# Average pooling by four: one 32 KB store for every two 64 KB loads

## The chip, the core and the metric

The kernel runs on one core of a Trainium2 chip. Its engines used here are VectorE (DVE in the profile), ScalarE (ACT) and SyncE (SP, which only issues DMAs); 16 DMA engines move data between HBM and the core's on-chip memory, SBUF, which has 128 partitions. The metric is the device time of one execution in microseconds, the median of several runs. Sizes such as "64 KB" are per partition; a 64 KB load is 128 x 64 KB = 8.389 MB, and a 16 KB store is 2.097 MB.

## The reference

The input is float32 of shape (64, 256, 8192), and every four neighbouring numbers are replaced by their mean; kernel size and stride are both 4:

```
out_len = (length - kernel_size) // stride + 1
for i in range(out_len):
    start = i * stride
    output[:, :, i] = np.mean(x[:, :, start : start + kernel_size], axis=2)
```

The output has shape (64, 256, 2048). 536.87 MB are read and 134.22 MB written, and nothing is used twice. Since 8192 is a multiple of 4, no window crosses a row, and the whole input can be treated as one flat array.

## The kernel before

The flat input is cut into blocks. A block of width w covers 128 x w neighbouring numbers, of which partition p gets the p-th run of w, so that a load of 64 KB a partition reads one solid stretch of 8.389 MB in HBM. There are 63 blocks of 16384 numbers a partition, and the last 16384 are cut into five blocks of 8192, 4096, 2048, 1280 and 768, which share one input buffer and one result buffer. In this text, load 0 to load 62 are the full blocks, and the pieces are the five small ones (the tail).

There are two input buffers of 64 KB (`xin`) and four result buffers of 16 KB (`res`), 192 KB in all.

For each block, `load` (line 62) issues one DMA on SP's queue. `means` then runs two additions on VectorE: line 71 adds even and odd neighbours, in place, into the first half of the input buffer; line 72 adds even and odd neighbours of those sums into the result buffer. ScalarE then multiplies the result by 1/4 in place (line 80); only for the last piece VectorE does that (line 76). `store` (line 85) issues a DMA of the result.

The loop runs over the blocks in order and issues load i + 1 before the sums of block i. Because there are two input buffers, load i + 1 can begin only when line 72 has read the last of block i - 1. The loads of all five pieces are issued together, once load 61's buffer is free. Most stores are issued by ScalarE itself, right behind the multiplication; the stores of load 62 and of the first piece are issued by SP, behind all the loads. No engine order is written out by hand beyond this program order; semaphores that the framework inserts hold an instruction until its operands are ready, and until a buffer's last reader is done.

Queue q1 in the profile holds what SP issues, and q10 what ScalarE issues.

Of the kernel before, what the change touches and what calls it, by code (L numbers as in the profile page):

```python
# [1 line left out]

# [4 lines left out]


FULL = 16384
BUFS_IN = 2  # L10
BUFS_OUT = 4

HEAD = ()
TAIL = (8192, 4096, 2048, 1280, 768)


@with_exitstack
def kernel(
    ctx: ExitStack,
    tc: tile.TileContext,  # L20
    x: bass.AP,
    kernel_size: bass.AP,
    stride: bass.AP,
    out: bass.AP,
):
    nc = tc.nc
    K, S = int(kernel_size), int(stride)
    assert K == S == 4
    B, C, L = x.shape
    assert L % K == 0  # L30
    P = nc.NUM_PARTITIONS
    dt = x.dtype
    add = mybir.AluOpType.add


    xf = x.rearrange("b c l -> (b c l)")
    of = out.rearrange("b c l -> (b c l)")
    rest = B * C * L // P - sum(HEAD) - sum(TAIL)
    assert rest % FULL == 0
    blocks = [(w, i == 0) for i, w in enumerate(HEAD)]  # L40
    blocks += [(FULL, True)] * (rest // FULL)
    blocks += [(w, i == 0) for i, w in enumerate(TAIL)]
    n = len(blocks)
    first = n - len(TAIL)

    pin = ctx.enter_context(tc.tile_pool(name="xin", bufs=BUFS_IN))
    pout = ctx.enter_context(tc.tile_pool(name="res", bufs=BUFS_OUT))

    xs, begins = {}, [0]
    for w, _ in blocks:  # L50
        begins.append(begins[-1] + w)

    def load(i):

        w, fresh = blocks[i]
        if fresh:
            load.tile, load.at = pin.tile([P, FULL], dt, name="xt"), 0
        a = load.at
        load.at += w
        src = xf[P * begins[i] : P * begins[i + 1]].rearrange("(p m) -> p m", p=P)  # L60
        xs[i] = load.tile[:, a : a + w]
        nc.sync.dma_start(out=xs[i], in_=src)  # L62

    def means(i):
        w, fresh = blocks[i]
        if fresh:
            means.tile, means.at = pout.tile([P, FULL // K], dt, name="ot"), 0
        a = means.at
        means.at += w // K
        o, xt = means.tile[:, a : a + w // K], xs.pop(i)  # L70
        nc.vector.tensor_tensor(out=xt[:, : w // 2], in0=xt[:, ::2], in1=xt[:, 1::2], op=add)  # L71
        nc.vector.tensor_tensor(  # L72
            out=o, in0=xt[:, : w // 2 : 2], in1=xt[:, 1 : w // 2 : 2], op=add
        )
        if i == n - 1:
            nc.vector.tensor_scalar(  # L76
                out=o, in0=o, scalar1=1.0 / K, scalar2=None, op0=mybir.AluOpType.mult
            )
        else:
            nc.scalar.mul(o, o, 1.0 / K)  # L80
        return o

    def store(engine, i, o):
        dst = of[P * begins[i] // K : P * begins[i + 1] // K]
        engine.dma_start(out=dst.rearrange("(p m) -> p m", p=P), in_=o)

    loaded = 0
    for i in range(n):

        while loaded < n and (loaded < i + BUFS_IN or loaded > first):  # L90
            load(loaded)
            loaded += 1
        o = means(i)

        store(nc.sync if i in (first - 1, first) else nc.scalar, i, o)


# [1 line left out]
_INS = ['x', 'kernel_size', 'stride']  # L99
_OUTS = [((64, 256, 2048), 'float32')]  # L100

_NUMBERS = {'kernel_size': 4, 'stride': 4}


# [26 lines left out]
```

## Time and profile before

| | us |
|---|---|
| time, median of 3 runs (1555.77 to 1555.85) | 1555.82 |
| the profiled execution's own time | 1555.85 |
| its span, first to last instruction | 1554.1 |
| VectorE busy | 840.5 |
| ScalarE busy | 233.1 |
| waits of VectorE on loads, in total | 700.5 |

In the profile, "L71" is line 71. A group's line has the engine, the operation, output and input with their shapes, the count, the busy time and the mean of one instruction in nanoseconds, and then the idle time of the engine before these instructions and what ended it. In the timeline and in the chain of waits, the first number of a line is the start in microseconds and the second the duration. A DMA's line has its size, and the time from its issue to its landing. Part 3 of the page gives, for a queue, packets, megabytes and the share of the 16 DMA engines' time that its packets took.

### The profile page before, as it was taken

The numbers are of one execution on the slowest core, as the hardware profiler recorded it, in microseconds if no ns is written. First come the engines' busy times: TensorE is split into PE (matmuls) and PEld (weight loads), VectorE is DVE, ScalarE is ACT, GpSimd is POOL, SyncE is SP. The second block draws the span as 40 slices with busy tenths as digits, with TensorE's granted clock in tenths as the row PEclk, the third lists the DMA queues.
The fourth block names the chain that finished last, engine by engine and source line by source line (L and its number), as shares of the span: only waits on it lengthen the run. The fifth ranks groups of instructions, "written<-read, shape, count | busy, mean of one in ns | idle before, by whom it ended". The sixth has DMA issues, their size and how long they took to land.

```text
span 1554.1 us, 576 instructions
## 1 busy us (share of the span) xinstructions
DVE 840.5 (54%) x137; ACT 233.1 (15%) x68; POOL 0.2 (0%) x4
## 2 busy tenths in 40 slices
DVE  3646556465464554645546455464554645646557
ACT  1111110110101101011011110111101111011111
POOL 0000000000000000000000000000000000000000
DMA  9999999999999999999999999999999999999999
GB/s 420 416 433 439 439 439 439 427 422 433 439 439 439 436 423 428 434 439 439 437 437 416 434 436 439 439 437 430 420 435 437 439 439 435 431 421 434 438 439 385
DMA packets 19589, 671.14 MB, mean 432 GB/s; under 512 B 2176, under 2 KB 2432, under 8 KB 2944
## 3 DMA queue, kind: packets, MB, share of 16 engines
q1 hardware_dynamic: 10080, 540.02, 80.3%
q10 hardware_dynamic: 9504, 131.08, 19.7%
q14 instruction: 5, 0.04, 0.0%
HBM read 536.87 MB, written 134.22 MB: 432 GB/s over the span
## 4 chain that ended last, share of the span: by engine, by line
DMA 72%; DVE 27%; issue 0%; DVEq 0%; SPq 0%
DMA xt<-in_x_dram 72%; DVE xt L71 18%; DVE ot L72 9%; DVEq L72 0%; SPq L62 0%; DVE ot L76 0%
## 5 line engine op out<-in xcount | busy, mean ns | idle before, releaser
L71 DVE TENSOR_TENSOR xt<-xt 128x8192 f32<-128x8192 f32 (+2 forms) x68 | 556.8, 8190 | 700.5 <-DMA xt<-in_x_dram 700.5
L80 ACT ACTIVATE ot<-ot 128x4096 f32<-128x4096 f32 (+2 forms) x67 | 231.8, 3461 | 1312.8 <-DVE ot L72 1312.8
L72 DVE TENSOR_TENSOR ot<-xt 128x4096 f32<-128x4096 f32 (+2 forms) x68 | 283.8, 4175 | 6.0 <-DVE xt L71 0.5
L80 ACT ACT_TABLE_LOAD x1 | 1.3, 1283 | 0.7 <-PEq L112 0.7
L76 DVE TENSOR_SCALAR ot<-ot 128x192 f32<-128x192 f32 x1 | 0.3, 261 | 0.0
L112 POOL MEMSET const-bfloat16-1.0<- 128x1 bf16 x1 | 0.1, 101 | 0.0
L112 POOL MEMSET const-uint8-127<- 128x1 uint8 x1 | 0.1, 101 | 0.0
L112 POOL MEMSET const-float32-0.0<- 128x1 f32 x1 | 0.1, 98 | 0.2 <-issue 0.2
L112 POOL MEMSET const-float32-1.0<- 128x1 f32 x1 | 0.1, 98 | 0.0
## 6 DMA issues: line engine op xcount, KB each, us to landing
out_dram<-ot ACTq DMA_DIRECT2D x62, 2048.0 KB, 31.6
xt<-in_x_dram SPq DMA_DIRECT2D x1, 4096.0 KB, 25.5
xt<-in_x_dram SPq DMA_DIRECT2D x1, 2048.0 KB, 30.1
out_dram<-ot SPq DMA_DIRECT2D x1, 2048.0 KB, 13.4
xt<-in_x_dram SPq DMA_DIRECT2D x1, 1024.0 KB, 32.1
out_dram<-ot SPq DMA_DIRECT2D x1, 1024.0 KB, 10.5
xt<-in_x_dram SPq DMA_DIRECT2D x63, 35.1
xt<-in_x_dram SPq DMA_DIRECT2D x1, 640.0 KB, 33.8
```

Of the source, the lines that this page charges most:

```text
L71: nc.vector.tensor_tensor(out=xt[:, : w // 2], in0=xt[:, ::2], in1=xt[:, 1::2], op=add)
L72: nc.vector.tensor_tensor(out=o, in0=xt[:, : w // 2 : 2], in1=xt[:, 1 : w // 2 : 2], op=add)
L76: nc.vector.tensor_scalar(out=o, in0=o, scalar1=1.0 / K, scalar2=None, op0=mybir.AluOpType.mult)
L80: nc.scalar.mul(o, o, 1.0 / K)
L112: nc = _bacc.Bacc("TRN2", target_bir_lowering=False, num_devices=1)
```

## The change

The first 62 loads are grouped in pairs. A pair covers 128 x 32768 neighbouring numbers, and partition p has a run of 32768 of them, 128 KB: the pair's first load reads the first 64 KB of every partition's run, the second load the second 64 KB. Input buffers and the two additions of each load stay as they are. Both loads of a pair write their sums into the two halves of one result buffer of 32 KB; after the second, one ScalarE instruction scales the whole of it, and one DMA stores 32 KB a partition, from ScalarE's queue. There are two such result buffers instead of four of 16 KB, so the memory used is the same 192 KB.

Load 62 stays single, with its own scaling and its store on SP's queue. The last 16384 numbers are one group as well: each partition has a run of 64 KB, and it is loaded in four pieces of 8192, 4096, 2560 and 1536 numbers, instead of five solid blocks. The four pieces are scaled and stored one by one, the first on SP's queue, the rest on ScalarE's; the last is again scaled by VectorE.

That is 67 loads instead of 68, and 36 stores instead of 68.

```
-BUFS_IN = 2
-BUFS_OUT = 4
+PAIR = 2
-TAIL = (8192, 4096, 2048, 1280, 768)
+TAIL = (8192, 4096, 2560, 1536)
...
+    sizes = [PAIR] * ((loads - 2) // PAIR)
+    sizes += [1] * (loads - PAIR * len(sizes))
+    begins = [sum(sizes[:g]) * FULL for g in range(len(sizes))]
+    pin = ctx.enter_context(tc.tile_pool(name="xin", bufs=2))
+    pout = ctx.enter_context(tc.tile_pool(name="res", bufs=2))
+
+    def part(flat, g, k):
+        a, n = begins[g] // k, sizes[g] * FULL // k
+        return flat[P * a : P * (a + n)].rearrange("(p m) -> p m", p=P)
+
+    def load(g, a, xt):
+        nc.sync.dma_start(out=xt, in_=part(xf, g, 1)[:, a : a + xt.shape[1]])
+
+    def store(engine, g, ot, a, b):
+        engine.dma_start(out=part(of, g, K)[:, a:b], in_=ot[:, a:b])
+
+    def sums(xt, o):
+        w = xt.shape[1]
         nc.vector.tensor_tensor(out=xt[:, : w // 2], in0=xt[:, ::2], in1=xt[:, 1::2], op=add)
         nc.vector.tensor_tensor(
             out=o, in0=xt[:, : w // 2 : 2], in1=xt[:, 1 : w // 2 : 2], op=add
         )
...
+    full = [(g, l) for g, n in enumerate(sizes[:-1]) for l in range(n)]
+    xs = {}
+
+    def fetch(i):
+        g, l = full[i]
+        xs[i] = pin.tile([P, FULL], dt, name="xt")
+        load(g, l * FULL, xs[i][:, :])
+
+    tail = len(sizes) - 1
+    edges = [sum(TAIL[:i]) for i in range(len(TAIL) + 1)]
+    fetch(0)
+    for i, (g, l) in enumerate(full):
+        if i + 1 < len(full):
+            fetch(i + 1)
+        else:
+            xt = pin.tile([P, FULL], dt, name="xt")
+            for a, b in zip(edges[:-1], edges[1:]):
+                load(tail, a, xt[:, a:b])
+        if l == 0:
+            ot = pout.tile([P, PAIR * FULL // K], dt, name="ot")
+        o = ot[:, l * FULL // K : (l + 1) * FULL // K]
+        sums(xs.pop(i)[:, :], o)
+        if l == sizes[g] - 1:
+            o = ot[:, : sizes[g] * FULL // K]
+            nc.scalar.mul(o, o, 1.0 / K)
+            queue = nc.sync if i == len(full) - 1 else nc.scalar
+            store(queue, g, ot, 0, sizes[g] * FULL // K)
+
+    ot = pout.tile([P, PAIR * FULL // K], dt, name="ot")
+    for i, (a, b) in enumerate(zip(edges[:-1], edges[1:])):
+        o = ot[:, a // K : b // K]
+        sums(xt[:, a:b], o)
+        if i == len(TAIL) - 1:
+            nc.vector.tensor_scalar(out=o, in0=o, scalar1=1.0 / K, scalar2=None, op0=mult)
         else:
             nc.scalar.mul(o, o, 1.0 / K)
+        store(nc.sync if i == 0 else nc.scalar, tail, ot, a // K, b // K)
```

More of the change, by code (lines that the diff above doesn't have):

```diff
@@ L9 @@
 FULL = 16384
-BUFS_IN = 2
-BUFS_OUT = 4
-HEAD = ()
-TAIL = (8192, 4096, 2048, 1280, 768)
+PAIR = 2
+TAIL = (8192, 4096, 2560, 1536)
 @with_exitstack
@@ L32 @@
     dt = x.dtype
-    add = mybir.AluOpType.add
+    add, mult = mybir.AluOpType.add, mybir.AluOpType.mult
     xf = x.rearrange("b c l -> (b c l)")
     of = out.rearrange("b c l -> (b c l)")
[L38 to L70, printed above, removed]
+    loads = B * C * L // P // FULL
+    assert loads * P * FULL == B * C * L and sum(TAIL) == FULL
+    sizes = [PAIR] * ((loads - 2) // PAIR)
[12 more added lines that the diff above has]
+        w = xt.shape[1]
         nc.vector.tensor_tensor(out=xt[:, : w // 2], in0=xt[:, ::2], in1=xt[:, 1::2], op=add)
@@ L74, in means @@
         )
[L75 to L78, printed above, removed]
+    full = [(g, l) for g, n in enumerate(sizes[:-1]) for l in range(n)]
[29 more added lines that the diff above has]
+            nc.vector.tensor_scalar(out=o, in0=o, scalar1=1.0 / K, scalar2=None, op0=mult)
         else:
             nc.scalar.mul(o, o, 1.0 / K)
[L81 to L95, printed above, removed]
+        store(nc.sync if i == 0 else nc.scalar, tail, ot, a // K, b // K)
 _INS = ['x', 'kernel_size', 'stride']
```

## The prediction

> **What bounds the kernel now.** I read the page's summary first, then the groups of instructions by shape, the waits, the start of the timeline, the DMA issues and the end of the chain.
>
> ```profile
> span 1554.1 us, 576 instructions
> DVE 840.5 (54%) x137; ACT 233.1 (15%) x68; POOL 0.2 (0%) x4
> q1 hardware_dynamic: 10080, 540.02, 80.3%
> q10 hardware_dynamic: 9504, 131.08, 19.7%
> HBM read 536.87 MB, written 134.22 MB: 432 GB/s over the span
> ```
>
> VectorE works 54% of the span, ScalarE 15%; the two DMA queues together take 80.3 + 19.7 = 100% of the 16 DMA engines. q1 holds SP's transfers (68 loads and two stores), q10 ScalarE's 66 stores. A DMA leaves 128 packets, one a partition row, and 16 small ones: 66 x 144 = 9504, 70 x 144 = 10080. So each DMA engine handles 8 rows of a load or store.
>
> ```profile
> DVE xt L71 <- DMA xt<-in_x_dram: 700.5, 64, 22.8
> L71 DVE TENSOR_TENSOR xt<-xt 128x8192 f32<-128x8192 f32 x63 | 547.6, 8692 | 699.1 <-DMA xt<-in_x_dram 699.1
> L72 DVE TENSOR_TENSOR ot<-xt 128x4096 f32<-128x4096 f32 x63 | 278.8, 4426 | 5.9 <-DVE xt L71 0.5
> L80 ACT ACTIVATE ot<-ot 128x4096 f32<-128x4096 f32 x63 | 227.8, 3616 | 1305.3 <-DVE ot L72 1305.3
> ```
>
> VectorE needs 8.69 + 4.43 = 13.1 us for a load, then waits on the next. No row has VectorE waiting for a result buffer.
>
> ```profile
> 22.76 8.69 DVE L71 TENSOR_TENSOR xt<-xt 128x8192 f32<-128x8192 f32 x1 [22.76 <-DMA xt<-in_x_dram]
> 35.95 3.62 ACT L80 ACTIVATE ot<-ot 128x4096 f32<-128x4096 f32 x1 [33.94 <-DVE ot L72]
> 42.09 8.69 DVE L71 TENSOR_TENSOR xt<-xt 128x8192 f32<-128x8192 f32 x1 [6.17 <-DMA xt<-in_x_dram]
> 1494.02 8.69 DVE L71 TENSOR_TENSOR xt<-xt 128x8192 f32<-128x8192 f32 x1 [10.98 <-DMA xt<-in_x_dram]
> 1518.21 8.69 DVE L71 TENSOR_TENSOR xt<-xt 128x8192 f32<-128x8192 f32 x1 [10.99 <-DMA xt<-in_x_dram]
> ```
>
> L71 starts as its load lands, so distances between starts are prices. Loads 0 to 1, before any store: 42.09 - 22.76 = 19.33 us for 8.389 MB, 434 GB/s. Loads 61 to 62, one store among them: 24.19 us for 10.486 MB, 433 GB/s; the commonest distance in the whole timeline is 24.18. Reads alone and reads with writes run at one rate: bytes are the bound. The page's rate has dips (427 and 422 in slices 7 and 8) that the landings don't have: the chain's steps there start at 284.28 and 332.64, two loads in 48.36 us.
>
> ```profile
> out_dram<-ot ACTq DMA_DIRECT2D x1, 2048.0 KB, 27.2
> out_dram<-ot ACTq DMA_DIRECT2D x62, 2048.0 KB, 31.6
> ```
>
> The first store (issues between 38 and 58 us) lands after 27.2 us, though its bytes alone are worth 4.85 us. That fits packets of the two queues taking turns: eight rounds of a 64 KB load row (19.33 / 8 = 2.42 us) and a 16 KB store row (0.61) are 24.2, and 3.0 are start and completion. At the median of 31.6, each store outlives the 24.2 us to the next one: the store queue is never empty.
>
> ```profile
> 1507.25 25.49 DMA xt<-in_x_dram
> 1532.77 4.44 DVE xt L71
> 1546.81 0.26 DVE ot L76
> out_dram<-ot ACTq DMA_DIRECT2D x1, 96.0 KB, 6.1
> ```
>
> At the end VectorE works without a break from 1532.77 to 1547.07, but the DMA engines still move 403 GB/s between 1543.6 and 1551.0: the last stores' bytes set the end. The last store, issued near 1547.1, lands 6.1 us later; on an emptier queue it would need about the 3.0 above, so VectorE is some 3 us early.
>
> **The change part by part**, against the profiled execution: span 1554.1, its time 1555.85, 1.75 outside the span; the median shown is 1555.82, so a change of the span is put onto that.
>
> *31 merged stores.* With c the time of 16 KB on an engine, o a packet's fixed cost, s that of completion: 32c + 8o + s = 19.33 and 8c + 8o + s = 24.18 - 19.33 = 4.85. So 24c = 14.48, 8c = 4.827, and a store's fixed cost on the engines is 0.023 us. 31 x 0.023 = 0.7 us saved. With the mean distance, (1518.21 - 42.09) / 61 = 24.20, the fixed cost is 0.05: 1.5 saved. On the other side, load 62 to the tail's first piece (eight rows each of 32 and 16 KB) took 1532.77 - 1518.21 = 14.56 where 3 x 4.827 + 2 x 0.023 = 14.53 was due; such an excess with every pair would cost 1 us. Ends: -1.5 and +1; taken -0.7, from the row that recurs some sixty times.
>
> The Trainium skill, page "DMA: Bandwidth & Descriptors", section "Anatomy of one DMA", gives a DMA issued from GpSimd a fixed 2.0 us beside its bytes. Charged to the 33 DMAs that go here (136 to 103), that would be 66 us, a time near 1490; the 0.023 above says that queued DMAs hide it, and I go by that row.
>
> *ScalarE.* 31 pairs of 3.62 us become 31 instructions on 128x8192: from 1.911 (2048 wide) to 3.616 (4096) a step costs 1.705, so 3.62 + 2 x 1.705 = 7.03 us. Busy time hardly moves; ScalarE idles 85%. The cost is delay: a pair's store is issued 13.1 + 7.0 = 20.1 us after its second load lands, its first half's bytes a load later than before. Behind the instruction ScalarE has only the store that needs it. Nothing, as long as the queues hold work.
>
> *Does the load queue hold work?* When no store is in flight a load takes 19.33 us, and the load after it is issued 13.1 us after its predecessor landed: 6.2 us to spare, of which a start with completion takes 22.76 - 0.73 - 19.33 = 2.7. 3.5 us are left. The start of this trace shows the case: load 2, issued behind load 0's sums, was behind load 1 without a gap (42.09 to 66.64 is 24.55 with a store among it). Nothing; without that cover each microsecond of gap costs 31 us.
>
> *Two result buffers of 32 KB.* A pair's store moves eight rounds of 64 and 32 KB: 8 x (2.42 + 1.21) = 29.0, plus 3.0: landed 20.1 + 32.0 = 52 us after the pair's second load. The buffer is written again by the pair after next, at L72 of its first load: three loads later (about 72.5) plus 8.7, 81 us. 29 us to spare: nothing.
>
> At the tail it is tight. The tail's buffer is that of the last pair. With T the landing of load 61, that store is issued at T + 20.1; load 62 lands near T + 21; from there 32 KB store rows alternate with the first piece's 32 KB rows, 8 x 2.42 = 19.4, so both finish near T + 41 and the store is known to have landed near T + 43. The piece's L72 comes at T + 41 + 4.4 = T + 45.5. 2 us to spare; a wait of up to 2 would eat into VectorE's 3 us. Nothing, bound +2.
>
> *The tail in four.* Old sums: 14.40 us of instructions. New, by interpolating the rows: 6.72 and 3.51 for the first two pieces, 1.48 + 0.82 for 2560, 0.95 + 0.55 for 1536, 0.45 for the scaling on VectorE: 14.48. VectorE ends 0.1 us later, under the stores. SP's order stays: four loads, then the store of load 62, then that of the first piece, each waiting on ScalarE with nothing behind. When the last load row lands, 4.19 MB of stores remain, as before: 9.7 us of DMA in both. One load and one store fewer: 0.05 us.
>
> *Loads from 128 KB rows.* 62 loads now read 64 KB of every 128 KB instead of one solid block. No row shows that. The nearest rows: 16 KB store rows at that pitch (431 GB/s), 32 KB at 32 (14.56 us above, 432), 64 KB at 64 (434): two doublings with no loss, so I take nothing. As upper end I charge each load the worst excess of one distance in the trace, 24.60 against 24.18: 62 x 0.42 = 26 us. On the other side a gain beyond 434 GB/s isn't seen anywhere.
>
> The same page, section "Latency and other measured facts", speaks against this part: rows at 512 KiB pitch gave 207 GB/s per direction, at 4 MiB 103, padded 214. Our pitch is below its list, so as written it charges nothing; read as a 3.3% loss that begins here, it would make 63 x 19.33 = 1218 us of loads 40 us longer, about 1595.
>
> Sum: -0.7 - 0.05 + 0.0, so a span near 1553.3 and 1555.1 by the median.
>
> **The rivals.**
> - *Doubled read pitch* (the slower side). For: it is the one thing the trace has no row for. Against: no loss over two doublings. It decides from a load longer by 3.1 / 62 = 0.05 us; at the bound, 1555.1 + 26 = 1581.
> - *The load queue runs dry once in a pair.* For: load-only phases are new. Against: 3.5 us of cover, and load 2. At 1 us of gap: 1555.1 + 31 = 1586.
> - *The tail's buffer wait.* It decides when the wait passes 3 us by the 3.1 that count: from 6 us; at 8, 1555.1 + 5 = 1560.
> - *Faster.* With every byte at 434 GB/s, 671.09 MB take 1546.3; with the head (22.76 - 19.33 = 3.4) and 2.2 for the last landing the span is 1551.9, the time 1553.6. More than 0.2% would need a rate that no row has.
> - *32 KB rows split into 16 KB packets,* so that the merge saves nothing: 1555.8. The packet count tells.
>
> **How the numbers follow.** 0.2%, 3.1 us, is about what can be told from no change: 1552.7 to 1558.9 is "same". The forecast with the split and small tail waits: 0.74, its own range 1553.5 to 1557. Pitch 0.14, dry queue 0.03, tail 0.03: slower 0.20. Faster 0.06. The range from 1552.5 to 1566 leaves out most of the 0.06 and about two thirds of the pitch and queue cases, some 0.17.
>
> **What would show it.** Packets 19589 down to 14837 (q10 34 x 144 = 4896, q1 69 x 144 = 9936). Distances between L71 starts alternate, near 20.5 and 27.8, summing to 48.3 a pair. The ScalarE group reads 128x8192, x31, about 7.0 us; a store of 4096 KB lands in about 32 us. No wait of L72 on a store but perhaps one at the tail, under 2 us. Wrong if the first two loads land over 19.4 us apart (pitch), if a pair's sum exceeds 48.5, or if the engines idle between pieces at the end.

## The result, and the profile after

The changed kernel takes 1571.32 us (1569.45 to 1571.62), the kernel before 1555.84: a ratio of 1.0097, 95% interval 1.0079 to 1.0114. It became 15.5 us slower, 1.0%, where no change was forecast. The profiled execution took 1571.62, its span is 1569.8.

The summary and the two DMA queues of the changed kernel's page:

```profile
span 1569.8 us, 477 instructions
DVE 840.7 (54%) x135; ACT 226.5 (14%) x36; POOL 0.2 (0%) x4
DMA packets 14835, 671.12 MB, mean 428 GB/s; under 512 B 1648, under 2 KB 1776, under 8 KB 2160
q1 hardware_dynamic: 9936, 540.02, 80.4%
q10 hardware_dynamic: 4896, 131.07, 19.3%
HBM read 536.87 MB, written 134.22 MB: 427 GB/s over the span
```

Work and bytes are the same and the DMA engines are as busy as before, but the rate over the span fell from 432 to 427 GB/s. The rows did arrive as 32 KB packets: 4896 records on q10 and 9936 on q1, as counted ahead.

Its groups by shape, its waits and a line of its DMA issues:

```profile
L60 DVE TENSOR_TENSOR xt<-xt 128x8192 f32<-128x8192 f32 x63 | 547.6, 8693 | 711.7 <-DMA xt<-in_x_dram 711.7
L61 DVE TENSOR_TENSOR ot<-xt 128x4096 f32<-128x4096 f32 x63 | 278.8, 4425 | 3.8
L91 ACT ACTIVATE ot<-ot 128x8192 f32<-128x8192 f32 x31 | 217.9, 7029 | 1308.5 <-DVE ot L61 1308.5
```
```profile
DVE xt L60 <- DMA xt<-in_x_dram: 716.1, 65, 22.9
DVE ot L61 <- DMA out_dram<-ot: 1.1, 1, 1.1
```
```profile
out_dram<-ot ACTq DMA_DIRECT2D x31, 4096.0 KB, 33.2
```

Nothing was added on an engine: VectorE waits 716.1 us for loads instead of 700.5, and these 15.6 us are the whole loss. No buffer is late but the tail's, by 1.1 us. So the loads come later, and the timeline tells where (L60 starts as its load lands; ACTq is the issue of a store):

```profile
22.87 8.69 DVE L60 TENSOR_TENSOR xt<-xt 128x8192 f32<-128x8192 f32 x1 [22.87 <-DMA xt<-in_x_dram]
42.21 8.69 DVE L60 TENSOR_TENSOR xt<-xt 128x8192 f32<-128x8192 f32 x1 [6.19 <-DMA xt<-in_x_dram]
61.56 8.69 DVE L60 TENSOR_TENSOR xt<-xt 128x8192 f32<-128x8192 f32 x1 [6.20 <-DMA xt<-in_x_dram]
...
627.63 8.69 DVE L60 TENSOR_TENSOR xt<-xt 128x8192 f32<-128x8192 f32 x1 [15.30 <-DMA xt<-in_x_dram]
647.87 0.34 ACTq L56 DMA_DIRECT2D out_dram<-ot  x1
648.15 8.69 DVE L60 TENSOR_TENSOR xt<-xt 128x8192 f32<-128x8192 f32 x1 [7.37 <-DMA xt<-in_x_dram]
676.82 8.69 DVE L60 TENSOR_TENSOR xt<-xt 128x8192 f32<-128x8192 f32 x1 [15.47 <-DMA xt<-in_x_dram]
```

The first three landings, before any store, are 19.34 and 19.35 us apart although they read 64 KB of every 128 KB: reads alone have lost nothing. Then the distances alternate. 648.15 - 627.63 = 20.52 is a load (19.33) and one 32 KB store row (1.21), and from 250 us on such short distances recur within a few hundredths. The load with the other seven store rows should take 19.33 + 8.47 = 27.8; it took 28.67 here and between 28.05 and 28.86 elsewhere from 250 us on. From load 3 (89.16) to load 61 (1508.22) the mean of a pair is 1419.06 / 29 = 48.93 us, where 2 x 24.18 = 48.36 was the price before: 0.57 a pair, 17 us over the 31 pairs (the total lost 15.5). The loss is in the load into which a store starts. In this text a *start* is a store that begins on a queue that stood empty.

The trace's DMA packet records put it more narrowly. A load row of 64 KB takes 2.42 us on its engine; in the kernel before, 65 of 8064 took over 0.03 us longer. In the changed kernel 586 did, with an excess of 14.5 us per engine (before: 1.3), most of it within 5 us of a store's first rows. The later rows, taking turns with store rows, run at 2.42 again.

### The profile page after: what moved, and what is told of

The parts are those of the page before. It is cut to its first block, busy times and chain, and to the rows that moved or that the text cites. A ratio compares the mean times of both kernels' runs of the same rounds, so it can differ in the third digit from the quotient of the medians.

```text
span 1569.8 us, 477 instructions
## 1 busy us (share of the span) xinstructions
DVE 840.7 (54%) x135; ACT 226.5 (14%) x36; POOL 0.2 (0%) x4
## 3 DMA queue, kind: packets, MB, share of 16 engines
q1 hardware_dynamic: 9936, 540.02, 80.4%
q10 hardware_dynamic: 4896, 131.07, 19.3%
## 4 chain that ended last, share of the span: by engine, by line
DMA 73%; DVE 26%; issue 0%; SPq 0%
DMA xt<-in_x_dram 73%; DVE xt L60 17%; DVE ot L61 9%; SPq L53 0%; DVE ot L101 0%
## 5 line engine op out<-in xcount | busy, mean ns | idle before, releaser
L60 DVE TENSOR_TENSOR xt<-xt 128x8192 f32<-128x8192 f32 (+2 forms) x67 | 556.8, 8310 | 716.1 <-DMA xt<-in_x_dram 716.1
L91 ACT ACTIVATE ot<-ot 128x8192 f32<-128x8192 f32 (+1 forms) x32 | 221.5, 6923 | 1322.1 <-DVE ot L61 1322.1
L103 ACT ACTIVATE ot<-ot 128x2048 f32<-128x2048 f32 (+2 forms) x3 | 3.7, 1235 | 11.4 <-DVE ot L61 11.4
## 6 DMA issues: line engine op xcount, KB each, us to landing
out_dram<-ot ACTq DMA_DIRECT2D x31, 4096.0 KB, 33.2
xt<-in_x_dram SPq DMA_DIRECT2D x1, 4096.0 KB, 24.2
```

## The experiments

Three theories came first. **Restart**: 16 load rows against 8 store rows let the store queue run empty once in a pair, and every fresh start costs. **Pitch**: taking 64 KB of every 128 KB is slower beside writes. **Row size**: 32 KB store rows are slower beside loads.

**e1_split_store**: the changed kernel, a pair's store as two of 16 KB rows.

```
-            store(queue, g, ot, 0, sizes[g] * FULL // K)
+            for h in range(sizes[g]):
+                store(queue, g, ot, h * FULL // K, (h + 1) * FULL // K)
```

> Three theories for the 0.56 us that a pair of loads costs more in the changed kernel (48.92 against 48.36 us between landings). Restart: the store queue now runs empty once in a pair, and every start of stores beside running loads costs the DMA engines about half a microsecond. Pitch: reading 64 KB of every 128 KB is slower beside writes. Row size: 32 KB store rows are slower beside loads than 16 KB ones. Here the changed kernel keeps its pairs, its one scaling and its pitch, but a pair's store is issued as two, each of 16 KB rows, right behind each other. There are then 16 store rows to 16 load rows on each DMA engine, so the store queue should hardly run empty. Restart: landings 48.36 us a pair again, time 1555 to 1557. Row size: the same, 1555 to 1557. Pitch: 1571.

1556.03 us (ratio 1.0001, 0.9992 to 1.0010). Its timeline, with the issue of two stores and three landings:

```profile
639.46 0.86 ACTq L56 DMA_DIRECT2D out_dram<-ot  x2
643.40 8.69 DVE L60 TENSOR_TENSOR xt<-xt 128x8192 f32<-128x8192 f32 x1 [11.03 <-DMA xt<-in_x_dram]
667.58 8.69 DVE L60 TENSOR_TENSOR xt<-xt 128x8192 f32<-128x8192 f32 x1 [10.97 <-DMA xt<-in_x_dram]
691.77 8.69 DVE L60 TENSOR_TENSOR xt<-xt 128x8192 f32<-128x8192 f32 x1 [11.04 <-DMA xt<-in_x_dram]
```

24.18 and 24.19, as before the change. Pitch, pairs, the one scaling and the tail in four pieces are all still there, so none of them costs by itself.

**e5_layout_alone**: each half scaled and stored by itself, in 16 KB rows, four buffers.

```
-            nc.scalar.mul(o, o, 1.0 / K)          # the pair's 32 KB
...
-            store(queue, g, ot, 0, sizes[g] * FULL // K)
...
+        nc.scalar.mul(o, o, 1.0 / K)              # each half
...
+        queue.dma_start(out=part(of, g, K)[:, l * FULL // K : (l + 1) * FULL // K], in_=o)
```

> The layout of the change alone: loads of 64 KB from every 128 KB and the tail in four pieces, but each half scaled and stored by itself, 16 KB rows at 32 KB pitch, four result buffers. The store queue is again always occupied. Restart: 1555 to 1557. Row size: 1555 to 1557. Pitch: 1571.

1555.83 (1.0000, 0.9990 to 1.0009). Pitch falls a second time. The Trainium skill's list of row pitches with a loss (page "DMA: Bandwidth & Descriptors", section "Latency and other measured facts") begins at 512 KiB; for the 64 KB rows of this case no loss reaches down to 128 KB.

**e2_half_loads**: the kernel before, each full load in two of 32 KB rows.

```
-        nc.sync.dma_start(out=xs[i], in_=src)
+        for h in range(0, w, w // 2 if w == FULL else w):
+            e = h + (w // 2 if w == FULL else w)
+            nc.sync.dma_start(out=xs[i][:, h:e], in_=src[:, h:e])
```

> The kernel before, each full load issued as two of 32 KB rows, so that a DMA engine has 16 load rows to 8 store rows; stores stay at 16 KB rows, no pitch is doubled in HBM beyond the old 64 KB. A store should then take 8 x (1.21 + 0.61) = 14.5 us of every 24.2 and the store queue run empty 62 times. Restart: 62 x 0.5 = 31 us longer, 1580 to 1590, half of that if a restart with 32 KB rows costs half. Pitch: 1556 to 1558. Row size: 1556 to 1558.

1560.17 (1.0028, 1.0017 to 1.0039): all three missed. The store queue did run empty (a store lands in 18.4 us, and the next is issued 24.25 later), but the loss of 4.3 us is far from 31.

```profile
626.47 8.69 DVE L73 TENSOR_TENSOR xt<-xt 128x8192 f32<-128x8192 f32 x1 [11.20 <-DMA xt<-in_x_dram]
643.38 0.34 ACTq L87 DMA_DIRECT2D out_dram<-ot  x1
650.73 8.69 DVE L73 TENSOR_TENSOR xt<-xt 128x8192 f32<-128x8192 f32 x1 [11.04 <-DMA xt<-in_x_dram]
```

24.26 against 24.18: 0.07 a load by the commonest distances, and 63 x 0.07 = 4.4 is the loss. It isn't the starts, as e6 shows below: there, loads with no store in flight take 19.43 in two parts and 19.34 in one. So a start as such is free, at least where it comes 7.35 us ahead of a landing and beside 32 KB load rows.

**e3_one_queue**: 32 KB rows, pitch and merged scaling kept, but pair stores issued by SP, after the next load.

```
-            store(queue, g, ot, 0, sizes[g] * FULL // K)
+            late.append((g, ot))
...
+        while late:                 # after the next fetch
+            g0, o0 = late.pop()
+            store(nc.sync, g0, o0, 0, sizes[g0] * FULL // K)
...
```

> The changed kernel with its 32 KB rows, its pitch and its merged scaling, but all pair stores issued by SP, behind the next load, so that loads and stores stand in one queue that never runs empty and no second queue takes turns with it. Restart: no start beside running loads, landings of about 48.3 us a pair, time 1555 to 1558. Pitch or row size, if they act wherever writes and reads meet: 1571, or nearly so; if every switch between reading and writing costs, 31 switches each way still cost and the time stays near 1571.

1559.22 (1.0021, 1.0012 to 1.0031). From 470 us on a pair has no loss: load and store run one after the other.

```profile
616.79 8.69 DVE L60 TENSOR_TENSOR xt<-xt 128x8192 f32<-128x8192 f32 x1 [6.14 <-DMA xt<-in_x_dram]
645.79 8.69 DVE L60 TENSOR_TENSOR xt<-xt 128x8192 f32<-128x8192 f32 x1 [15.85 <-DMA xt<-in_x_dram]
665.13 8.69 DVE L60 TENSOR_TENSOR xt<-xt 128x8192 f32<-128x8192 f32 x1 [6.13 <-DMA xt<-in_x_dram]
```

29.00 + 19.34 = 48.34 us a pair. The 3.3 us were lost elsewhere. Before 470 us most pairs take 48.55 to 49.0, why is open; against e12 below, which has no loss in its pairs, load 62 lands 3.2 us later (1516.32 against 1513.16), and the whole span is 4.1 us longer. The tail can account for the rest of that: its first piece waits on the last pair's store, which now stands behind more loads:

```profile
DVE ot L61 <- DMA out_dram<-ot: 7.3, 1, 7.3
```

So in some twenty pairs on end neither 32 KB rows nor switches between reading and writing cost anything on one queue. The Trainium skill (same page, section "Issuing engines are not separate DMA queues") says that issuing from several engines only saves issue time, since all DMAs share the 16 engines. Here one queue was 0.6 us a pair cheaper than the changed kernel's two; e8 and e12 below reach the same on two queues, so it isn't the queue by itself.

What was left: 64 KB load rows, 32 KB store rows, two queues, a start. A fourth theory came from the timeline of the changed kernel. Its store is issued 0.28 us ahead of a landing. **Boundary**: a start is costly when it comes together with the end of a load. Against it stood **load row** (64 KB rows are held up at any start) and **store row** (32 KB rows do it).

**e6_after_half_loads**: the changed kernel with each full load in two of 32 KB rows.

```
-        load(g, l * FULL, xs[i][:, :])
+        for h in (0, FULL // 2):
+            load(g, l * FULL + h, xs[i][:, h : h + FULL // 2])
```

> So far: no cost where the store queue is always occupied, none with one queue, and only 0.07 us a start where load rows are 32 KB and store rows 16 KB. Open is what a start of stores costs by. Load row: a load row of 64 KB that is under way when the second queue wakes up is what gets held up. Store row: it needs the 32 KB store row. Boundary: it needs a start that falls together with the end of a load, as it does in the changed kernel (store issued at 647.87, next load landed at 648.15). Here the changed kernel has each full load in two of 32 KB rows: 31 starts, at the same moment, store rows of 32 KB. Load row: landings about 48.4 us a pair, 1556 to 1559. Store row: 48.9, about 1571. Boundary: 48.9, about 1571.

1560.24 (1.0028, 1.0017 to 1.0038), near the expectation of load row. A pair takes 29.05 + 19.44 = 48.49, and 2 x 0.07 of that is the price of the second DMA that e2 shows: no cost of a start is left with 32 KB load rows, though the store is issued 0.8 us after a landing:

```profile
625.57 8.69 DVE L60 TENSOR_TENSOR xt<-xt 128x8192 f32<-128x8192 f32 x1 [15.83 <-DMA xt<-in_x_dram]
645.01 8.69 DVE L60 TENSOR_TENSOR xt<-xt 128x8192 f32<-128x8192 f32 x1 [6.28 <-DMA xt<-in_x_dram]
645.82 0.34 ACTq L56 DMA_DIRECT2D out_dram<-ot  x1
674.06 8.69 DVE L60 TENSOR_TENSOR xt<-xt 128x8192 f32<-128x8192 f32 x1 [15.85 <-DMA xt<-in_x_dram]
```

Early in the changed kernel's own trace two starts, behind its first, come 0.9 us after a landing with 64 KB load rows; their pairs took 49.75 and 48.72, 1.4 and 0.4 us too long.

**e7_every_other_store**: the kernel before, 31 of its stores left out.

```
-        store(nc.sync if i in (first - 1, first) else nc.scalar, i, o)
+        if i >= first - 1 or i % 2:
+            store(nc.sync if i in (first - 1, first) else nc.scalar, i, o)
```

> The kernel before with every second full result not stored (31 of the 62 stores before load 62 are left out, the additions and scalings stay), so that 64 KB load rows meet a store queue of 16 KB rows that runs empty 31 times, a start coming 16.8 us after a landing. Bytes alone: 2 x 19.33 + 4.85 = 43.51 us for two loads, time 1556 - 31 x 4.85 = 1405.6. Load row: about 44.0 for two loads, time near 1420. Store row: 43.5, time 1404 to 1408. Boundary: 43.5, since a start 16.8 us after a landing comes about 2.5 us ahead of the next one.

1405.94; 43.5 us for two loads. No cost of starts, so load row falls as a sufficient cause. The distances are 19.3 and 24.2, so all eight store rows fall into one load, and the issue is 2.4 us ahead of a load's end, the place of e9 below. A start there is free with 16 KB store rows.

**e8_late_store**: the changed kernel, a pair scaled twice by 1/2, the start 7 us later.

```
-            nc.scalar.mul(o, o, 1.0 / K)
+            if sizes[g] == PAIR:
+                nc.scalar.mul(o, o, 0.5)
+                nc.scalar.mul(o, o, 0.5)
+            else:
+                nc.scalar.mul(o, o, 1.0 / K)
```

> The changed kernel with a pair scaled by two ScalarE instructions of 1/2 each, 7.03 us apiece, so that a store starts 7 us later, in the middle of a load instead of at the end of one; nothing else changes. Boundary: 48.4 us a pair, 1555 to 1558. Load row and store row: 48.9 us a pair, 1570 to 1572.

1554.98 (0.9994, 0.9985 to 1.0004). Of the three only Boundary allows this: rows, queues, pitch, merging and the number of starts are those of the changed kernel, and the whole loss is gone.

```profile
620.20 8.69 DVE L60 TENSOR_TENSOR xt<-xt 128x8192 f32<-128x8192 f32 x1 [12.21 <-DMA xt<-in_x_dram]
643.12 8.69 DVE L60 TENSOR_TENSOR xt<-xt 128x8192 f32<-128x8192 f32 x1 [9.77 <-DMA xt<-in_x_dram]
647.50 0.34 ACTq L56 DMA_DIRECT2D out_dram<-ot  x1
668.54 8.69 DVE L60 TENSOR_TENSOR xt<-xt 128x8192 f32<-128x8192 f32 x1 [12.21 <-DMA xt<-in_x_dram]
```

The issue is 4.4 us after a landing instead of 0.3 ahead of one; 22.92 + 25.42 = 48.34. More work on ScalarE made the kernel 16 us faster.

**e9_early_store**: each half scaled as soon as it is summed, one 32 KB store, 3.4 us earlier.

```
         sums(xs.pop(i)[:, :], o)
+        nc.scalar.mul(o, o, 1.0 / K)
         if l == sizes[g] - 1:
-            o = ot[:, : sizes[g] * FULL // K]
-            nc.scalar.mul(o, o, 1.0 / K)
```

> The changed kernel with each half scaled by itself right after its sums (two ScalarE instructions of 3.62 us a pair), and one store of 32 KB rows behind the second, issued 16.7 instead of 20.1 us after the landing and so about 2.5 us before the next load's end. Boundary: less, 1555 to 1565. Load row and store row: 48.9 us a pair, 1570 to 1572.

1580.25, with executions from 1561.64 to 1582.5 (ratio 1.0130, 1.0073 to 1.0187). In the profiled one, the 1561.64, twenty pairs behind the first take 48.36 on average and the last nine 49.0. The distances are 19.3 and 29.0, so again all eight store rows fall into one load. One and the same place can be free for twenty pairs and then costly, and its cost differs from one execution to the next.

Four more starts, e10 to e13, were then placed between, by an extra ScalarE multiplication by 1 on part of the pair:

```
             nc.scalar.mul(o, o, 1.0 / K)
+            if sizes[g] == PAIR:
+                nc.scalar.mul(ot[:, :1160], ot[:, :1160], 1.0)     # 1160, 2620, 4096, 5525
```

> A start of stores 7 us later cost nothing, 3.4 us earlier cost 1561 to 1582 from one execution to the next. Two readings are left of where a start is costly. Load's end: a start close to the end of a load costs. Row rhythm: a load row takes 2.42 us on an engine, and what counts is the place in that rhythm at which the start falls, whatever the row. Here the changed kernel has one more ScalarE instruction on a pair, a multiplication by 1 of 1160 columns, that starts the store 1.2 us later, half a row: issued 0.9 us after the next landing instead of 0.3 before it. Load's end: still near 1571, at least above 1560. Row rhythm: 1555 to 1558.

> The same with 2620 columns: 2.4 us later, a whole row. Load's end: cheaper than the changed kernel, 1555 to 1562. Row rhythm: 1570 to 1573 as in the changed kernel.

> The same with 4096 columns: 3.65 us later, a row and a half. Load's end: 1555 to 1557. Row rhythm: 1555 to 1557. If it lies at 1570 both are wrong and only a start at a particular place is cheap.

> The same with 5525 columns: 4.84 us later, two whole rows. Load's end: 1555 to 1557. Row rhythm: 1570 to 1573.

| run | start later by, us | issue after the nearest landing, median of the profiled execution | time (executions) |
|---|---|---|---|
| e9 | -3.4 | -2.5 | 1580.25 (1561.64 to 1582.50) |
| changed kernel | 0 | -0.3 | 1571.32 (1569.45 to 1571.62) |
| e10 | 1.2 | 0.9 | 1566.01 (1559.58 to 1568.56) |
| e11 | 2.4 | 0.9 | 1560.03 (1556.67 to 1562.69) |
| e12 | 3.65 | 2.2 | 1554.89 (1554.67 to 1555.23) |
| e13 | 4.84 | 3.3 | 1555.13 (1555.03 to 1555.72) |
| e8 | 7.06 | 4.4 | 1554.98 (1554.84 to 1555.21) |

The third column lags behind the second, since a later start also moves the landings by whole store rows of 1.21 us. In e10 it goes to and fro between -0.3 and 0.9, in e11 between 0.7 and 2.1; the profiled executions of both are among their fastest (1559.58 and 1557.59). Row rhythm is out: 1.2 us, half a row, still cost 10, and 2.4 and 4.84, whole rows, cost 4 and nothing.

The times came as Load's end expected: the cost falls as the start is delayed, and from 3.65 us on there is none. The landings don't bear out its reason. In one execution of e10, a start just ahead of a landing is free and one farther from it is not:

```profile
622.84 8.69 DVE L60 TENSOR_TENSOR xt<-xt 128x8192 f32<-128x8192 f32 x1 [13.56 <-DMA xt<-in_x_dram]
644.28 0.34 ACTq L56 DMA_DIRECT2D out_dram<-ot  x1
644.54 8.69 DVE L60 TENSOR_TENSOR xt<-xt 128x8192 f32<-128x8192 f32 x1 [8.55 <-DMA xt<-in_x_dram]
672.36 8.69 DVE L60 TENSOR_TENSOR xt<-xt 128x8192 f32<-128x8192 f32 x1 [14.60 <-DMA xt<-in_x_dram]
692.88 8.69 DVE L60 TENSOR_TENSOR xt<-xt 128x8192 f32<-128x8192 f32 x1 [7.37 <-DMA xt<-in_x_dram]
693.80 0.34 ACTq L56 DMA_DIRECT2D out_dram<-ot  x1
720.87 8.69 DVE L60 TENSOR_TENSOR xt<-xt 128x8192 f32<-128x8192 f32 x1 [14.78 <-DMA xt<-in_x_dram]
741.39 8.69 DVE L60 TENSOR_TENSOR xt<-xt 128x8192 f32<-128x8192 f32 x1 [7.37 <-DMA xt<-in_x_dram]
```

The start at 644.28, 0.26 ahead of a landing, is followed by 27.82 + 20.52 = 48.34, no cost; the one at 693.80, 0.92 after a landing, by 27.99 + 20.52 = 48.51. Over the whole trace nine starts 0.2 to 0.3 us ahead of a landing cost nothing, at the place that costs the changed kernel 0.6 us a pair. In e11 the sixteen starts 0.7 to 0.9 after a landing are free, and the thirteen at 2.1 cost 0.2 on average, a place where e12 pays nothing.

What goes with the cost is the load that lands just ahead of the start. Where it took at most 20.6 us, so that at most one row of the previous store fell into it, 78 of 88 starts cost over 0.1 us; where it took 21.5 or more, with two rows or more, 3 of 115 did (changed kernel, e8 and e10 to e14, without the first and the last pair's store). In e9 it takes 19.3, and 10 of 29 starts cost. No run varies this by itself, so why it goes with the cost is open.

Nor does a store reach the engines at the landing: by the packet records its first rows begin 3.4 to 7.2 us after the issue, in the changed kernel some 3 to 7 us behind the landing.

The fastest, e12:

```profile
643.02 8.69 DVE L60 TENSOR_TENSOR xt<-xt 128x8192 f32<-128x8192 f32 x1 [8.42 <-DMA xt<-in_x_dram]
645.34 0.34 ACTq L56 DMA_DIRECT2D out_dram<-ot  x1
669.62 8.69 DVE L60 TENSOR_TENSOR xt<-xt 128x8192 f32<-128x8192 f32 x1 [13.39 <-DMA xt<-in_x_dram]
691.36 8.69 DVE L60 TENSOR_TENSOR xt<-xt 128x8192 f32<-128x8192 f32 x1 [8.59 <-DMA xt<-in_x_dram]
```

26.60 + 21.74 = 48.34. Its packet records have 63 late load rows and 2.1 us of excess, where the changed kernel has 586 and 14.5. Against the kernel before its ratio is 0.9994 (0.9984 to 1.0003); the interval holds 1, yet its ten executions (1554.67 to 1555.23) all lie below the 25 of the kernel before on the same chip (1555.68 to 1556.45).

Two last runs asked whether a costly start needs the 32 KB store rows or the pitch, since e7 had neither.

**e14_solid_loads**: the pitch taken away.

```
-        nc.sync.dma_start(out=xt, in_=part(xf, g, 1)[:, a : a + xt.shape[1]])
+        src = part(xf, g, 1)[:, a : a + xt.shape[1]]
+        if sizes[g] == PAIR:
+            at = P * (begins[g] + a)
+            src = xf[at : at + P * FULL].rearrange("(p m) -> p m", p=P)
+        nc.sync.dma_start(out=xt, in_=src)
```

> The changed kernel, but the loads of a pair read solid blocks of 8.389 MB as in the kernel before, while the stores keep their 32 KB rows; the means of a pair therefore land in other places of the output than the reference has them, with the same number of bytes. Store row: a start near a load's end is costly whatever the pitch, 1566 to 1575. Pitch: 1555 to 1557.

1571.25 (1.0095, 1.0078 to 1.0112), the time of the changed kernel to 0.1 us, with the store at the same place:

```profile
627.59 8.69 DVE L64 TENSOR_TENSOR xt<-xt 128x8192 f32<-128x8192 f32 x1 [15.28 <-DMA xt<-in_x_dram]
647.83 0.34 ACTq L60 DMA_DIRECT2D out_dram<-ot  x1
648.13 8.69 DVE L64 TENSOR_TENSOR xt<-xt 128x8192 f32<-128x8192 f32 x1 [7.39 <-DMA xt<-in_x_dram]
676.34 8.69 DVE L64 TENSOR_TENSOR xt<-xt 128x8192 f32<-128x8192 f32 x1 [15.01 <-DMA xt<-in_x_dram]
```

**e15_half_store**: the 32 KB rows taken away.

```
-            store(queue, g, ot, 0, sizes[g] * FULL // K)
+            store(queue, g, ot, (sizes[g] - 1) * FULL // K, sizes[g] * FULL // K)
```

> The changed kernel, but of a pair only the second half of the result is stored, rows of 16 KB, issued at the same moment after the same scaling (31 halves of 2.097 MB are left out). Without any cost of a start: two loads and one 16 KB store in 43.5 us, time 1555 - 31 x 4.85 = 1405. Store row: 1404 to 1407. Pitch: 1415 to 1425.

1405.14, no cost at all:

```profile
628.28 8.69 DVE L60 TENSOR_TENSOR xt<-xt 128x8192 f32<-128x8192 f32 x1 [6.79 <-DMA xt<-in_x_dram]
628.59 0.34 ACTq L56 DMA_DIRECT2D out_dram<-ot  x1
651.86 8.69 DVE L60 TENSOR_TENSOR xt<-xt 128x8192 f32<-128x8192 f32 x1 [10.37 <-DMA xt<-in_x_dram]
671.80 8.69 DVE L60 TENSOR_TENSOR xt<-xt 128x8192 f32<-128x8192 f32 x1 [6.78 <-DMA xt<-in_x_dram]
```

671.80 - 628.28 = 43.52 us for two loads and a store, with an issue 0.3 us after a landing, and at most one store row in the load ahead of it (19.9 us). At that place 32 KB store rows cost the changed kernel 0.6 us, and 16 KB rows cost nothing: the 32 KB store row is needed, the pitch is not.

Shown, then: the loss is paid where stores of 32 KB rows start on the second queue beside 64 KB load rows, and only if they start at certain times. One queue (e3, over its last twenty pairs), 32 KB load rows (e6), 16 KB store rows (e15) or a start 3.65 us or more later (e12, e13, e8) takes the loss away. That the store queue must have stood empty is likely but not shown by itself: e1, which keeps it occupied, also has 16 KB rows. What makes a moment costly is open; the distance to the next landing alone does not decide it. That 64 KB load rows are stretched near a start is seen in the packet records; why, no run tells.

## Why the prediction was wrong

- **The step that failed** is the term of the 31 merged stores. It took a store's whole price from rows in which the store queue never runs empty, c, o and s from the distance of 24.18, and so knew no price for a start. It gave -0.7 us with ends of -1.5 and +1; the loss of 17 us in the pairs lies far outside. In its place the runs showed a price of a start: 0.57 us in each pair (48.93 against 48.36), which e8 removes by a later start alone. The saving of 0.7 may be there: e12 is 1 us below the kernel before (1554.89 against 1555.87). But the mean of a pair shows none of it, 48.39 us in both, so where that 1 us lies is open.
- **The row that should have bounded it was read and passed over.** The trace of before has one start of stores beside running loads, store 0, issued 2.5 us ahead of the landing at 42.09, and the next distance is 24.55, 0.37 above the usual. The prediction used it to show that the load queue has no gap. As the price of a start, 31 x 0.37 = 11.5 us, it would have put the upper end of this term near 1567 and made a start a rival with a price. Such a bound would have been right by luck, for the 0.37 us are probably another effect. The first store costs extra in every run with starts, also where later ones are free: 0.7 us in e7 (24.93 + 19.30 against 43.52), 1.0 in e12 (26.55 + 22.75 against 48.34).
- **The load queue and the buffers** held as worked out. 20.52 us between landings with a load issued in time, no wait on a result buffer but 1.1 us at the tail (up to 2 was allowed), a pair's store in 33.2 us (32). e3, where that store comes later, shows the tail's wait at 7.3.
- **ScalarE, the packets, the alternation** came as said: 7.029 us (7.03), 4896 and 9936 packets, 20.5 and about 28.4 us (20.5 and 27.8). The sum of a pair was the sign named for a wrong forecast, "exceeds 48.5", and it is 48.93.
- **The doubled pitch**, the rival with the largest chance, is refuted by e1, e5 and e14. The slower side had the right sign for the wrong reason.
- **"Bytes are the bound"** was right but not enough: a pair with the same bytes takes 48.93 us in the changed kernel and 48.34 in e8, where only the second queue's start is later.

## What to carry to other kernels

When two DMA queues share the engines, count packets on both sides: equal numbers kept the second queue always occupied here, and a merge that halved one side made it stop and start. That was free with 16 KB store rows and with 32 KB load rows, and cost 17 us with 32 KB store rows beside 64 KB load rows, started when the changed kernel starts them. A start has a place in time, and its price depends on it, so move it by a few microseconds before giving up the merge. To find such a cost, compare the landings of a pair in the middle of the trace with the price of its bytes; the first start is a poor guide, since it cost extra in every run. A time that varies between executions can be another sign.

## What was not expected of the hardware

- A delay made the kernel faster: 3.65 us more of ScalarE in a pair is worth 16 us, and 3.4 us less costs up to 11 more.
- The cost is not the same in each pair or execution: e9 at one and the same start took 1561.64 to 1582.5 us.
- Starts 0.3 us ahead of a landing cost 0.6 us each in the changed kernel and nothing in e10.
- Splitting a 64 KB load into two DMAs costs 0.07 to 0.09 us a load (19.43 against 19.34 with no store in flight), three to four times the 0.023 that the prediction worked out for a 16 KB store.
